# A transformer's opening, regrouped by feature tiles: x first, squares summed on TensorE, six projections fed one tile of x at a time

## The chip, the cores and the metric

One core of a Trainium2 chip runs the whole program. The metric is the device time of one execution in microseconds. TensorE (PE) multiplies, VectorE (DVE) and ScalarE (ACT) do elementwise work, GpSimd (POOL) does a little of it, and SyncE (SP) only issues transfers. "PEld" is the loading of a matmul's stationary operand.

## The reference, cut to what matters

The reference is a chain of transformer layers on 256 rows of 1024 features. Only the first lines of the first layer matter here:

```
cond = silu(c)
mod  = cond @ ada_w[0] + ada_b[0]              # 6 x 1024: shift, scale, gate, ...
shift_m, scale_m, gate_m, ... = split(mod, 6)
h    = rmsnorm(x, g) * (1 + scale_m) + shift_m
proj = h @ attn_w_in[0]                        # qa ka va qb kb vb, 512 wide each
qa, ka = partial_rope(qa, positions), partial_rope(ka, positions)
...                                            # two attentions, output projection, feed-forward, further layers
```

Every weight is used once, so all of them are read from memory in the order of use. `rmsnorm` needs the sum of squares of a row over all 1024 features.

## The kernel before

Activations lie transposed: a tile holds 128 features (partitions) by 256 rows (columns), so x is eight tiles `self.x[k]`, each 128x512, of which the right half is scratch. The list `PLAN` names all weight units in order of use. A unit is up to 128x1024 float32 (512 KB). "mat" units are weights of a projection: ACT writes a rounded copy `h` (L378), DVE the remainder `l` (L379), and `mm3` multiplies with three matmuls per 128x128 block (L405 to L407: weight-high by activation-high, weight-high by activation-low, weight-low by activation-high), each streaming 256 columns. "mod" units are eighths of a modulation vector, stored transposed: one DVE operation (L491) multiplies a 128x1024 unit by the broadcast row `cond` and sums along the row, which gives 128 values as one column.

`pump` issues the loads on SP's queue, up to 12 units ahead, into a ring of nine buffers (`raw`); a buffer is free again when its unit has been used (mod) or split into `h` and `l` (mat). Split units wait in a ring of five. `get` takes the next mat unit, and `flush` works off the mod units that stand ahead of it.

A planner orders the instructions of each engine when the program is built: it issues what its own timing model finds ready, and the program order is only a preference. Semaphores are placed after that, so each engine runs its list strictly in order on the chip.

The opening runs like this. `build` loads the column constants, the broadcast `cond` row (512 KB), the broadcast positions, constants with an all-ones matrix, and x on ACT's queue behind the `cond` activation. `rope_tables` makes sine and cosine on DVE and ACT. `push` squares each x tile on ACT and adds up on POOL and DVE; two matmuls with `ones` finish the sum (L558, L559). `rsq` turns it into 1/rms `r` (two table functions on ACT, three DVE operations). `flush(KT)` works off eight mod units for the scale, `scale` makes x·gain·r (L853), `flush` works off eight more for the shift, `shift` makes the high and low parts of h (L860, L861). Then `moba_proj` makes the projections qa and ka for four head pairs, 24 matmuls each, and rotates each (copy L753, a matmul with `rot1` L755, DVE L756, POOL L757, DVE add, and for q `headsplit`). `vproj` makes va (L413 to L415, 48 matmuls of 512 columns). Attention, the second group and the output projection follow; the feed-forward part begins at about 180 us.

PSUM has eight banks: three tagged "mm", four "ax", one "nm". The tag "u" (four tiles) holds the intermediates of the rope tables and of the rotations.

Of the kernel before, what the change touches and what calls it, by code (L numbers as in the profile page):

```python
# [13 lines left out]
OP = mybir.AluOpType  # L14
# [74 lines left out]
def plan():  # L89
# [81 lines left out]
def _col_plan():  # L171
    o = 0
    for name, n in (("norm_mix_g", 16), ("norm_ffn_g", 16), ("ada_b", 96), ("final_norm_g", 8),
                    ("gdn_conv", 96), ("gdn_norm_g", 1), ("a_log", 1), ("dt", 1),
                    ("b_mod_2", 144), ("ffn1_norm_2", 16), ("mix_norm_2", 16), ("ffn2_norm_2", 16),
                    ("final_norm_2", 8), ("conv_w_2", 12), ("q_norm_2", 6), ("kv_norm_2", 4),
                    ("inv_freq", 1)):
        COLS[name] = (o, n)
        o += n
    return o  # L180
# [5 lines left out]
def pack_cols(i):  # L186
# [5 lines left out]
    def lay(v):  # L192
# [9 lines left out]
        "final_norm_g": _vec(i["final_norm_g"]), "gdn_conv": conv1, "gdn_norm_g": _vec(i["gdn_norm_g"][0]),  # L202
        "a_log": pad(i["gdn_a_log"][0]), "dt": pad(i["gdn_dt_bias"][0]),
        "b_mod_2": lay(i["b_mod_2"]), "ffn1_norm_2": lay(i["ffn1_norm_2"]), "mix_norm_2": lay(i["mix_norm_2"]),
# [6 lines left out]
def constants():  # L211
# [3 lines left out]
    c["ident"] = np.eye(128)  # L215
    c["ones"] = np.ones((128, 128))
    c["triu"] = (p[:, None] <= p[None, :]) * 1.0
# [41 lines left out]
    for g in range(2):  # L259
# [13 lines left out]
CONST = constants()  # L273
CONST_GROUPS = (("ident", "ones", "triu", "half", "rot1"),
                ("tril", "trimid", "upper", "m_causal", "m_sb", "m_lev"),
# [24 lines left out]
class Builder:  # L300
# [59 lines left out]

    def pump(self):
        nc = self.nc
        while self.pd < min(len(PLAN), self.pos + self.LOOK):
# [28 lines left out]
    def flush(self, n=len(PLAN)):  # L392

        end = self.pos + n
        while self.pos < min(end, len(PLAN)) and PLAN[self.pos][0] != "mat":
            self.pump()
            r = self.raw.pop(self.pos)
            self.mod_unit(PLAN[self.pos][1], r)
            self.pos += 1
# [69 lines left out]
    def condition(self, n, t):  # L469
# [4 lines left out]
        return t  # L474

    def conditions(self):

        self.conds[1:] = [self.condition(n, self.t("cnd")) for n in (1, 2)]

    def mod_unit(self, key, r):  # L480
# [12 lines left out]
        if m == KT - 1:  # L493
            o, _ = COLS["ada_b" if ns == 1 else "b_mod_2"]
            nch = 6 if ns == 1 else 9
            b = self.cols[:, o + (l * nch + ch) * 8:o + (l * nch + ch) * 8 + 8]
            for s in range(ns):
                v = t[:, 8 * s:8 * s + 8]
                nc.vector.tensor_tensor(v, v, b, op=OP.add)
                if ns == 2 and ch in (2, 8):  # L500
                    nc.vector.tensor_scalar(v, v, 0.5, None, op0=OP.mult)

    def gain(self, name, l, gname, ch):
# [22 lines left out]

    def stats(self, total=KT, gains=None):


        return {"gains": gains, "acc": None, "first": {}, "n": {}, "total": total, "p": {}}  # L530

    def push(self, st, src, c0, c1):
# [148 lines left out]
    def rope_tables(self):  # L681
        nc = self.nc
        pi = self.t("u", dt=I32)
        nc.scalar.dma_start(pi, bass.AP(tensor=self.a["pos"].tensor, offset=self.a["pos"].offset,
                                        ap=[[0, 128], [1, T]]))
        ang, kk, rr = self.t("u"), self.t("u"), self.t("u")
        nc.vector.tensor_copy(kk, pi)
        o = COLS["inv_freq"][0]
        nc.vector.tensor_scalar(ang, kk, self.cols[:, o:o + 1], None, op0=OP.mult)
        tab = self.t("tab")  # L690
# [52 lines left out]

    def moba_proj(self, h):
        nc = self.nc
        cos, sin = self.rope
        qz, ks = [], []
        for m in range(4):
            pq = self.gemm(self.get(("qa", m)), h, 0, T)
            pk = self.gemm(self.get(("ka", m)), h, 0, T)  # L750
            for p, i in ((pq, 0), (pk, 1)):
                t, u = self.t("u"), self.t("u")
# [12 lines left out]
        self.c = self.load_consts(1, "cst1")  # L765
        return qz, ks, self.vproj("va", h)

# [80 lines left out]

    def scale(self, st, A):

        r = self.rsq(st["p"][0], 1.0 / D)
        for k, x in enumerate(self.x):
            self.nc.vector.scalar_tensor_tensor(x[:, T:], x[:, :T], A[:, k:k + 1], r, op0=OP.mult, op1=OP.mult)  # L853

    def shift(self, B):

        h = [self.pair("h", T) for _ in range(KT)]
        for k, (hi, lo) in enumerate(h):
            t, b = self.x[k][:, T:], B[:, k:k + 1]
            self.nc.scalar.activation(hi, t, AF.Identity, bias=b)  # L860
            self.nc.vector.scalar_tensor_tensor(lo, t, b, hi.bitcast(F32), op0=OP.add, op1=OP.subtract)  # L861
        return h

    def attention(self, B, gate):
        h = self.shift(B)
        qa = self.moba_proj(h)
        P, oa, ob, ze = {}, [], [], {}
# [544 lines left out]
    def build(self):  # L1412
# [4 lines left out]
        right = es1.enter_context(self.tc.tile_pool(name="cond", bufs=1, side="right"))  # L1417
        self.conds = [self.condition(0, right.tile([128, D], F32, name="cond")), None, None]
        self.phase("attn")
        self.rope = self.rope_tables()  # L1420
        g0 = self.load_consts(0, "cst0")
        self.c0 = g0
        self.ident, self.ones, self.triu = g0["ident"], g0["ones"], g0["triu"]
        self.pump()
        self.x = []
        for k in range(KT):
            t = self.xp.tile([128, 512], F32, name=f"x{k}")
            nc.scalar.dma_start(t[:, :T], a["xT"][:, k])
            self.x.append(t)
        self.eps = {}  # L1430
        for e in (EPS, EPS * EPS):
            self.eps[e] = self.keep(1, f"eps{e}")
            nc.vector.memset(self.eps[e], e)
        self.table(LOG_SET)
        st = self.stats()
        for k in range(KT):
# [21 lines left out]
        for l in range(2):  # L1458
# [3 lines left out]
            else:  # L1462
                self.flush(KT)
                self.scale(st, self.gain("ada_w", 0, "norm_mix_g", 1))
                self.flush()
                st = self.attention(self.mod["ada_w", 0, 0], lambda: self.mod["ada_w", 0, 2])
            self.dump(f"x{2 * l}")
# [95 lines left out]
```

## Time and profile before

| | us |
|---|---|
| median of 3 runs | 2498.66 (2496.10 to 2502.42) |
| the profiled execution | 2497.55 |
| its span, first to last instruction | 2495.7 |
| PE busy | 2391.3 (96%) |
| PE weight loads busy | 2130.3 (85%) |
| DVE busy | 1786.3 (72%) |
| ACT busy | 1073.5 (43%) |
| POOL busy | 169.9 (7%) |

The span is split into busy shares by engine, so an average hides stages: here PE is busy nearly all the time except in the first stretch. Matmuls overlap one another in the pipeline, so the distance from start to start, not the duration shown, tells what one costs.

### The profile page before, as it was taken

The numbers are of one execution on the slowest core, as the hardware profiler recorded it, in microseconds if no ns is written. First come the engines' busy times: TensorE is split into PE (matmuls) and PEld (weight loads), VectorE is DVE, ScalarE is ACT, GpSimd is POOL, SyncE is SP. The second block draws the span as 40 slices with busy tenths as digits, with TensorE's granted clock in tenths as the row PEclk, the third lists the DMA queues.
The fourth block names the chain that finished last, engine by engine and source line by source line (L and its number), as shares of the span: only waits on it lengthen the run. The fifth ranks groups of instructions, "written<-read, shape, count | busy, mean of one in ns | idle before, by whom it ended". The sixth has DMA issues, their size and how long they took to land.

```text
span 2495.7 us, 38415 instructions
## 1 busy us (share of the span) xinstructions
PE 2391.3 (96%) x14963; PEld 2130.3 (85%) x14963; DVE 1786.3 (72%) x3087; ACT 1073.5 (43%) x1879; POOL 169.9 (7%) x172
## 2 busy tenths in 40 slices
PE   3999998899999999999999999999999999999998
PEld 2889998898999888888886888888988878988998
DVE  8987779886897997763657597663687663675765
ACT  3554455566644622223537432223432223456444
POOL 1000000414100100000010100000100000111000
PEclk9999999999999999999999999999999999999999
DMA  9766676432786475542220265452365452242652
GB/s 332 271 223 227 225 236 225 153 102 90 263 265 209 161 236 191 173 162 99 79 79 33 85 219 178 153 182 87 109 201 180 160 175 95 83 131 77 205 183 70
DMA packets 118406, 412.21 MB, mean 165 GB/s; under 512 B 13136, under 2 KB 16464, under 8 KB 118224
## 3 DMA queue, kind: packets, MB, share of 16 engines
q1 hardware_dynamic: 113904, 402.28, 47.7%
q10 hardware_dynamic: 4320, 7.47, 0.9%
q8 instruction: 118, 1.93, 0.3%
q14 instruction: 64, 0.52, 0.1%
HBM read 408.66 MB, written 1.05 MB: 164 GB/s over the span
## 4 chain that ended last, share of the span: by engine, by line
PE 76%; DVE 9%; DMA 8%; issue 3%; ACT 2%; POOL 1%; DVEq 0%; ACTq 0%; SPq 0%; POOLq 0%
PE pmm L405 21%; PE pmm L406 21%; PE pmm L407 21%; DMA r<-w 7%; DVE l L379 2%; DVE r L491 2%; DVE junk L491 2%; PE pax L1026 2%; PE pmm L1348 1%; PE pax L407 1%; PE pax L406 1%; PE pax L405 1%; PE pnm L1387 1%; PE pax L1358 1%; ACT h L378 1%
## 5 line engine op out<-in xcount | busy, mean ns | idle before, releaser
L378 ACT CAST h<-r 128x1024 fp32r<-128x1024 f32 (+2 forms) x543 | 549.6, 1017 | 992.4 <-PE pmm L406 907.3
L379 DVE TENSOR_TENSOR l<-r,h 128x1024 fp32r<-128x1024 f32 (+2 forms) x543 | 645.0, 1192 | 195.6 <-ACT h L378 188.2
L405 PE MATMUL pmm<-h,h 128*128 128x512 f32 (+1 forms) x1916 | 668.3, 350 | 31.3 <-ACT h L860 23.1
L406 PE MATMUL pmm<-h,h 128*128 128x512 f32 (+1 forms) x1916 | 664.7, 347 | 1.8 <-DVE h L593 1.6
L407 PE MATMUL pmm<-h,l 128*128 128x512 f32 (+1 forms) x1916 | 662.3, 346 | 0.0
L405 PEld LDWEIGHTS pmm<-h,h 128*128 128x128 f32 x1916 | 364.1, 190 | 78.1 <-ACT h L860 23.8
L406 PEld LDWEIGHTS pmm<-h,h 128*128 128x128 f32 x1916 | 364.2, 190 | 48.5 <-DVE h L593 3.7
L407 PEld LDWEIGHTS pmm<-h,l 128*128 128x128 f32 x1916 | 364.2, 190 | 44.7 <-issue 0.2
L405 PE MATMUL pmm<-hid,h 128*128 128x256 f32 (+1 forms) x1053 | 349.8, 332 | 6.2 <-DVE s L633 2.7
L406 PE MATMUL pmm<-hid,h 128*128 128x256 f32 (+1 forms) x1053 | 348.3, 331 | 1.5 <-DVE hid L444 1.5
L407 PE MATMUL pmm<-hid,l 128*128 128x256 f32 (+1 forms) x1053 | 348.0, 331 | 0.7 <-DVE l L379 0.7
L405 PE MATMUL pmm<-hb,h 128*128 128x258 f32 x1008 | 286.4, 284 | 5.7 <-ACT hb L581 4.2
L407 PE MATMUL pmm<-hb,l 128*128 128x258 f32 x1008 | 284.9, 283 | 0.0
L406 PE MATMUL pmm<-hb,h 128*128 128x258 f32 x1008 | 284.9, 283 | 0.0
L491 DVE SCALAR_TENSOR_TENSOR junk<-r,cnd 128x1024 f32<-128x1024 f32 x144 | 175.9, 1221 | 125.9 <-DMA r<-w 122.6
L405 PEld LDWEIGHTS pmm<-hid,h 128*128 128x128 f32 x1053 | 200.4, 190 | 26.3 <-ACT hid L443 3.9
L406 PEld LDWEIGHTS pmm<-hid,h 128*128 128x128 f32 x1053 | 200.4, 190 | 20.9 <-DVE hid L444 2.4
L407 PEld LDWEIGHTS pmm<-hid,l 128*128 128x128 f32 x1053 | 200.5, 190 | 19.3 <-DVE l L379 1.1
L405 PEld LDWEIGHTS pmm<-hb,h 128*128 128x128 f32 x1008 | 190.8, 189 | 7.3 <-ACT hb L581 5.0
L406 PEld LDWEIGHTS pmm<-hb,h 128*128 128x128 f32 x1008 | 191.7, 190 | 0.4 <-DVE hb L582 0.2
L407 PEld LDWEIGHTS pmm<-hb,l 128*128 128x128 f32 x1008 | 191.7, 190 | 0.1
L491 DVE SCALAR_TENSOR_TENSOR r<-r,cnd 128x1024 f32<-128x1024 f32 x144 | 176.1, 1223 | 5.5 <-ACT cnd L464 2.4
(332 smaller groups left out, 2867.8 us busy)
## 6 DMA issues: line engine op xcount, KB each, us to landing
r<-w SPq DMA_DIRECT2D x665, 512.0 KB, 4.2
r<-w SPq DMA_DIRECT2D x96, 448.0 KB, 3.4
r<-w SPq DMA_DIRECT2D x16, 256.0 KB, 2.5
cnd<-cond ACTq DMA_DIRECT2D x8, 512.0 KB, 4.6
r<-w SPq DMA_DIRECT2D x6, 384.0 KB, 3.2
const<-const SPq DMA_DIRECT2D x2, 960.0 KB, 6.3
x<-xT ACTq DMA_DIRECT2D x8, 128.0 KB, 5.7
x<-ctxT ACTq DMA_DIRECT2D x8, 128.0 KB, 2.6
```

The lines of the kernel that those rows point to most:

```text
L378: nc.scalar.copy(h[:, :n], r[:, :n])
L379: nc.vector.tensor_tensor(lo[:, :n], r[:, :n], h[:, :n].bitcast(F32), op=OP.subtract)
L405: nc.tensor.matmul(out, wh, ah, start=start, stop=False)
L406: nc.tensor.matmul(out, wh, al, start=False, stop=False)
L407: nc.tensor.matmul(out, wl, ah, start=False, stop=stop)
L491: nc.vector.scalar_tensor_tensor(o, r, 1.0, self.conds[ns - 1 + s], op0=OP.mult, op1=OP.mult, accum_out=t[:, 8 * s + m:8 * s + m + 1])
L1026: nc.tensor.matmul(p[:, s], a[:, s], b[:, s], start=True, stop=True)
L1348: self.nc.tensor.matmul(s, q, k, start=True, stop=True)
L1358: self.nc.tensor.transpose(p[:, 128 * b:128 * b + 128], P[:, 128 * b:128 * b + 128], self.ident)
L1387: nc.tensor.matmul(o[64 * a:64 * a + 64, 128 * qt:128 * qt + 128], V[2 * s + b][:, h], pts[a][:, 128 * b:128 * b + 128], start=b == 0, sto ...
```

## The change

The plan's first 24 units become eight groups of three: a mod unit for scale (eighth m), a "modk" unit for shift (all 1024 inputs by 128 outputs, not transposed), and a mat unit "first" m that holds, for feature tile m, the 128x128 blocks of six projections (qa and ka of head pairs 0 to 2). The bytes are the same as before. `first_tiles` walks the eight tiles of x: it works off the two modulation units, makes h for this tile, splits it, and adds the tile's product to all six projections, which stay open in six PSUM banks. `mod_cols` makes the shift column with eight small matmuls (the condition as a 128x32 stationary operand, 128 columns streamed, four column groups of the array), a copy on ACT, a matmul with `ones` and an ACT addition. The squares of x are summed by eight matmuls with `ones`. x·r goes to POOL. The `cond` row and the positions are loaded as single rows and spread over the partitions by matmuls; `ones` is written by a memset; x's loads are issued first, half on each of two queues; the constants of group 0 are loaded at the third tile, and the rope tables come after the six projections. The 24 mod units of the stage that follows are spread over 26 mat units instead of 32.

```diff
 def plan():
-    u = A(0, 1, 0)
     a = "attn_w_in"
-    q = []
+    u, q = [], []
+    for m, scale in enumerate(A(0, 1)):
+        u.append(scale)
+        u.append(("modk", ("ada_w", 0, 0, m), [("ada_w", 0, kt * 128, m * 128, 128) for kt in range(KT)]))
+        u.append(("mat", ("first", m), [(a, 0, m * 128, c + i * 128, 128) for i in range(3) for c in (0, 512)]))
     for s, base in (("a", 0), ("b", 1536)):
-        for m in range(4):
+        for m in range(0 if base else 3, 4):
...
-    u += _evenly(q, A(0, 2, 3, 4), 4, 0)
+    u += _evenly(q, A(0, 2, 3, 4), 2, 0)
...
+    def spread_row(self, p, row):
+        self.nc.tensor.matmul(p, self.ones[0:1, :], row, start=True, stop=True)
...
+    def mod_cols(self, key, r):
...
+        p = self.ax()
+        for kt in range(KT):
+            g = 32 * (kt % 4)
+            nc.tensor.matmul(p[g:g + 32, :128], self.cond0[:, kt, :], r[:, kt * 128:kt * 128 + 128],
+                             start=kt < 4, stop=kt >= 4)
+        e = self.t("u")
+        nc.scalar.copy(e[:, :128], p[:, :128])
+        nc.tensor.matmul(p[:, 256:264], e[:, :128], self.ones[:, :8], start=True, stop=True)
+        o = COLS["ada_b"][0] + m
+        nc.scalar.activation(self.mod[key[:3]][:, m:m + 1], p[:, 256:257], AF.Identity, bias=self.cols[:, o:o + 1])
...
     def push(self, st, src, c0, c1):
+        if st["tensor"]:
+            n = st["n"][0] = st["n"].get(0, 0) + 1
+            if n == 1:
+                st["p"][0] = self.psum("nm", 1)[:, :T]
+            nc.tensor.matmul(st["p"][0], self.ones, s[:, :T], start=n == 1, stop=n == tot)
+            return
...
-    def moba_proj(self, h):
+    def moba_proj(self, st):
+        h, ps = self.first_tiles(st)
+        self.rope = self.rope_tables()
         for m in range(4):
-            pq = self.gemm(self.get(("qa", m)), h, 0, T)
-            pk = self.gemm(self.get(("ka", m)), h, 0, T)
-            for p, i in ((pq, 0), (pk, 1)):
+            if m == 3:
+                ps += [self.gemm(self.get((n, m)), h, 0, T) for n in ("qa", "ka")]
+            for p, i in ((ps[2 * m], 0), (ps[2 * m + 1], 1)):
...
+    def first_tiles(self, st):
         r = self.rsq(st["p"][0], 1.0 / D)
+        for x in self.x:
+            nc.gpsimd.tensor_tensor(x[:, T:], x[:, :T], r, op=OP.mult)
+        ps = [(self.ax if i % 2 else self.mm)()[:, :T] for i in range(6)]
+        h = []
         for k, x in enumerate(self.x):
+            self.flush()
+            t, (hi, lo) = self.t("t"), self.pair("h", T)
+            nc.scalar.activation(t, x[:, T:], AF.Identity, scale=self.scale0[:, k:k + 1],
+                                 bias=self.mod["ada_w", 0, 0][:, k:k + 1])
+            h.append(self.split(t, hi, lo))
+            u = self.get(("first", k))
+            if k == 2:
+                self.c0.update(self.load_consts(0, "cst0"))
+                self.ident, self.triu = self.c0["ident"], self.c0["triu"]
+            for i, p in enumerate(ps):
+                self.mm3(p, u, i, hi, lo, k == 0, k == KT - 1)
+        return h, ps
...
 def build(self):
+        rows = [self.t("og")[0:1, :] for _ in range(2)]
+        for i in range(2):
+            nc.scalar.dma_start(rows[i], a["cond"][0:1, 512 * i:512 * i + 512])
+        self.x = []
+        for k in range(KT):
+            t = self.xp.tile([128, 512], F32, name=f"x{k}")
+            (nc.sync if k % 2 else nc.scalar).dma_start(t[:, :T], a["xT"][:, k])
+            self.x.append(t)
+        self.pump()
+        for i in range(2):
+            p = self.mm()
+            self.spread_row(p, rows[i])
+            self.act(self.conds[0][:, 512 * i:512 * i + 512], p, AF.Silu)
...
         self.table(LOG_SET)
-        st = self.stats()
+        st = self.stats(tensor=True)
```

## Rows read from the trace of the kernel before

**Rows 1.** The page: busy tenths of PE, DVE and DMA in 40 equal slices.
```profile
PE   3999998899999999999999999999999999999998
DVE  8987779886897997763657597663687663675765
DMA  9766676432786475542220265452365452242652
```

**Rows 2.** The chain that ended last, opening: start, duration, what.
```profile
7.48 5.15 DMA x<-xT
...
32.15 1.14 DVE r L491 x2
...
43.97 0.09 DVE mod_ada_w L499
44.08 0.52 ACT h L860
44.64 1.01 PE pmm L405 x3
```

**Rows 3.** Busy time by stretch: PE, PEld, DVE, ACT, POOL, PEclk, DMA share, GB/s.
```profile
0.00:44.64 44.64, 2.07 (x4) 1.17 (x4) 33.05 (x70) 13.61 (x22) 4.97 (x9) 1.00 0.95 351
20.00:35.00 15.00, 1.55 (x4) 0.67 (x2) 14.57 (x34) 5.07 (x8) 0.00 (x0) 1.00 1.03 411
44.64:49.30 4.66, 4.66 (x20) 4.38 (x21) 4.66 (x10) 3.68 (x8) 0.00 (x0) 1.00 0.91 323
49.30:73.17 23.87, 23.87 (x189) 23.25 (x188) 23.23 (x37) 10.70 (x18) 6.05 (x6) 1.00 0.89 324
73.17:84.90 11.73, 11.73 (x52) 9.47 (x51) 11.03 (x18) 5.19 (x7) 2.20 (x2) 1.00 0.91 302
84.90:180.00 95.10, 89.58 (x681) 82.28 (x679) 83.64 (x161) 51.93 (x99) 4.38 (x5) 1.00 0.63 227
```

**Rows 4.** DVE by line, 8.9 to 44.64 us: busy, mean ns, idle before.
```profile
L491 DVE SCALAR_TENSOR_TENSOR r<-r,cond 128x1024 f32<-128x1024 f32 x16 | 19.4, 1216 | 8.0 <-DMA r<-w 8.0
L379 DVE TENSOR_TENSOR l<-r,h 128x1024 fp32r<-128x1024 f32 x4 | 4.8, 1216 | 0.0
L853 DVE SCALAR_TENSOR_TENSOR x<-x,gain_ada_w,r 128x256 f32<-128x256 f32 x8 | 3.2, 474 | 0.0
L491 DVE DVE_READ_ACCUMULATOR r<-r,cond 128x1 f32 x16 | 1.3, 80 | 0.0
```

**Rows 5.** By stretch, instructions on tile u alone (rope tables).
```profile
0.00:44.64 44.64, 0.00 (x0) 0.00 (x0) 6.54 (x17) 0.83 (x2) 0.00 (x0) 1.00 0.95 351
```

**Rows 6.** ACT and POOL by shape, 0 to 200 us.
```profile
L860 ACT ACTIVATE h<-x,mod_ada_w 128x256 fp32r<-128x256 f32 x8 | 3.3, 494 | 6.1 <-DVE mod_ada_w L499 6.1
L464 ACT ACTIVATE y<-pnm,eps1e-06_155 128x256 f32<-128x256 f32 x2 | 1.0, 476 | 0.0
L757 POOL TENSOR_TENSOR u<-u,tab 128x256 f32<-128x256 f32 x8 | 8.3, 1031 | 48.7 <-PE pax L755 48.6
```

**Rows 7.** The chain, 66 to 185 us: full float32 matmuls of 256 columns.
```profile
66.31 0.43 PE pax L755 x2
...
183.39 0.85 PE pnm L558 x2
```

**Rows 8.** Busy time by stretch around the end of attention.
```profile
180.00:182.40 2.40, 0.09 (x2) 0.01 (x1) 2.40 (x5) 2.40 (x7) 1.03 (x1) 1.00 0.91 314
182.40:186.00 3.60, 3.60 (x13) 3.24 (x14) 3.60 (x12) 3.57 (x9) 0.00 (x0) 0.53 0.64 228
```

**Rows 9.** PE in order of time: six float32 matmuls, two column groups.
```profile
99.91 0.43 PE L739 MATMUL pax<-pt,v 128*64 128x128 f32 x2
...
100.67 0.38 PE L741 MATMUL pax<-pt,v 128*64 128x128 f32 x2
100.98 0.33 PE L803 MATMUL pax<-const,pz 128*128 128x128 f32 x1
```

**Rows 10.** Opening in order of time: the first weight unit's use.
```profile
8.93 1.23 DVE L491 SCALAR_TENSOR_TENSOR r<-r,cond 128x1024 f32<-128x1024 f32 x1 [8.03 <-DMA r<-w]
```

More of the change, by code (lines that the diff above doesn't have):

```diff
@@ L273 @@
 CONST = constants()
-CONST_GROUPS = (("ident", "ones", "triu", "half", "rot1"),
+CONST_GROUPS = (("ident", "triu", "half", "rot1"),
                 ("tril", "trimid", "upper", "m_causal", "m_sb", "m_lev"),
@@ L358, in ax, with pump @@
         return self.psum("ax", 4)
-    def pump(self):
+    def pump(self, look=LOOK):
         nc = self.nc
-        while self.pd < min(len(PLAN), self.pos + self.LOOK):
+        while self.pd < min(len(PLAN), self.pos + look):
             n, i = WIDTH[self.pd], self.pd
@@ L492, in mod_unit @@
                                            accum_out=t[:, 8 * s + m:8 * s + m + 1])
-        if m == KT - 1:
+        if key[:3] == ("ada_w", 0, 1):
+            o, g = COLS["ada_b"][0] + KT + m, COLS["norm_mix_g"][0] + m
+            nc.vector.scalar_tensor_tensor(self.scale0[:, m:m + 1], t[:, m:m + 1], self.bias1[:, m:m + 1],
+                                           self.cols[:, g:g + 1], op0=OP.add, op1=OP.mult)
+        elif m == KT - 1:
             o, _ = COLS["ada_b" if ns == 1 else "b_mod_2"]
@@ L501, in mod_unit @@
                     nc.vector.tensor_scalar(v, v, 0.5, None, op0=OP.mult)
+    def mod_cols(self, key, r):
+        nc = self.nc
+        m = key[3]
+        if m == 0:
+            self.mod[key[:3]] = self.keep(KT, "mod_first")
+        p = self.ax()
[8 more added lines that the diff above has]
+        nc.scalar.activation(self.mod[key[:3]][:, m:m + 1], p[:, 256:257], AF.Identity, bias=self.cols[:, o:o + 1])
     def gain(self, name, l, gname, ch):
@@ L525, in rsq, with stats @@
         return r
-    def stats(self, total=KT, gains=None):
-        return {"gains": gains, "acc": None, "first": {}, "n": {}, "total": total, "p": {}}
+    def stats(self, total=KT, gains=None, tensor=False):
+        return {"tensor": tensor, "gains": gains, "acc": None, "first": {}, "n": {}, "total": total, "p": {}}
     def push(self, st, src, c0, c1):
@@ L683, in rope_tables @@
         pi = self.t("u", dt=I32)
[L684 to L685 removed]
+        nc.scalar.dma_start(pi[0:1, :], self.a["pos"])
         ang, kk, rr = self.t("u"), self.t("u"), self.t("u")
[L687 removed]
+        nc.vector.tensor_copy(kk[0:1, :], pi[0:1, :])
+        p = self.ax()[:, :T]
+        self.spread_row(p, kk[0:1, :])
         o = COLS["inv_freq"][0]
[L689 removed]
+        nc.vector.tensor_scalar(ang, p, self.cols[:, o:o + 1], None, op0=OP.mult)
         tab = self.t("tab")
@@ L847, in sb_weights, with attention @@
         self.act(z, z, AF.Exp)
-    def scale(self, st, A):
+    def first_tiles(self, st):
+        nc = self.nc
         r = self.rsq(st["p"][0], 1.0 / D)
+        for x in self.x:
+            nc.gpsimd.tensor_tensor(x[:, T:], x[:, :T], r, op=OP.mult)
+        ps = [(self.ax if i % 2 else self.mm)()[:, :T] for i in range(6)]
+        h = []
         for k, x in enumerate(self.x):
[L853 to L866, printed above, removed]
+            self.flush()
[10 more added lines that the diff above has]
+        return h, ps
+    def attention(self, st, gate):
+        qa, h = self.moba_proj(st)
         P, oa, ob, ze = {}, [], [], {}
@@ L1417, in build @@
         right = es1.enter_context(self.tc.tile_pool(name="cond", bufs=1, side="right"))
-        self.conds = [self.condition(0, right.tile([128, D], F32, name="cond")), None, None]
         self.phase("attn")
[L1420 to L1429, printed above, removed]
+        self.ones = self.keep(128, "ones")
+        nc.gpsimd.memset(self.ones, 1.0)
+        self.cond0 = self.t("og")[:, :32 * KT].rearrange("p (k c) -> p k c", k=KT)
+        nc.gpsimd.memset(self.cond0, 0.0)
         self.eps = {}
@@ L1433, in build @@
             nc.vector.memset(self.eps[e], e)
+        rows = [self.t("og")[0:1, :] for _ in range(2)]
[7 more added lines that the diff above has]
+        self.pump()
+        self.conds = [right.tile([128, D], F32, name="cond"), None, None]
+        for i in range(2):
+            p = self.mm()
+            self.spread_row(p, rows[i])
+            self.act(self.conds[0][:, 512 * i:512 * i + 512], p, AF.Silu)
+        o = COLS["c"][0]
+        self.act(self.cond0[:, :, 0], self.cols[:, o:o + KT], AF.Silu)
+        self.scale0, self.bias1 = self.keep(KT, "scale0"), self.keep(KT, "bias1")
+        o = COLS["ada_b"][0] + KT
+        nc.vector.tensor_scalar(self.bias1, self.cols[:, o:o + KT], 1.0, None, op0=OP.add)
+        self.c0 = {}
         self.table(LOG_SET)
-        st = self.stats()
+        st = self.stats(tensor=True)
         for k in range(KT):
@@ L1462, in build @@
             else:
[L1463 to L1466, printed above, removed]
+                st = self.attention(st, lambda: self.mod["ada_w", 0, 2])
             self.dump(f"x{2 * l}")
```

9 lines of the change are left out of this document (4 added, 5 removed).

## The prediction, made before the change was run

> **What bounds the kernel now.** I read the page's busy tenths first: PE is at 8 or 9 in every slice but the first, where it is at 3 while DVE and DMA are at 8 and 9 [rows 1]. So the program is PE's, apart from one hole at its start. The chain of waits shows what the hole consists of: x lands at 12.6, then squares, DVE's modulation products, and the last of them (L499) frees ACT's first h at 44.08 and PE's first projection at 44.64 [rows 2]. The stretches say who works meanwhile: up to 44.64 PE is busy 2.07 us, DVE 33.05 [rows 3]; DVE's idle time is nearly all before its first product at 8.93, the landing of the first weight unit [rows 4, 10]. From there DVE is the limit, with 16 products (19.4 us) and the rope tables (6.54) [rows 4, 5]. Transfers run at 411 GB/s at most, 351 in the mean [rows 3]. From 44.64 on PE has no gap until 84.90, and up to 180 only 5.5 us; DVE is almost as full there, 23.23 of 23.87, then 11.03 of 11.73, then 83.64 of 95.10 [rows 3]. That second fact decides how much of an earlier start survives.
>
> **The change part by part: what must land.** The bytes of the first 24 units are 2816 columns per group, 1.44 MB, eight groups 11.5 MB. Ahead of them stand the column constants (0.23 MB) and x (1.05 MB); the 512 KB `cond` row, the 128 KB positions and 257 KB of constants ahead of the units are gone or moved. Before, 0.23 + 0.26 + 0.51 + 0.13 MB and the first unit, 1.64 MB, were in at 8.93 [rows 10]. Now 1.80 MB precede the same moment, 0.16 MB more, 0.4 us at 411 GB/s: first unit at 9.3, x complete at about 8. SP's queue issues four x loads ahead of its first unit; that is in this shift. One group takes 3.52 us at 411 GB/s; the third unit of group 0 lands at 11.5, of group 7 at 36.6 with the 0.2 MB of constants moved behind group 2. By before's mean of 351 GB/s the 12.9 MB take 36.7, the same. The ring of nine holds three groups, and its oldest unit must be used before the tenth load goes; DVE, which frees it, needs per group one product (1.22 + 0.08), a remainder of 768 columns (0.9, from the 1.22 of 1024), the low part of h (about 0.4, as L853's) and a gain column, together 2.7 us against 3.52 [rows 4]. So transfers are not held back.
>
> **The sum of squares.** Before, POOL and DVE added. Now PE does, eight float32 matmuls of 256 columns: 0.43 each at the upper level of the clock, 0.85 at the lower [rows 7]. From the landing of the first x (about 5.5) they end at 9 to 13; I take the lower level, 13. The two spreads of the `cond` row, 512 columns, cost by the same rows 0.85 to 1.7 each and lie before, while x is on its way; without that cover they would add 3.4. Then `rsq`: five dependent operations at most 0.48 each [rows 6], 2.5 with hand-overs: r at 15.5. POOL's first x·r takes 0.8 to 1.03 [rows 6], ACT's two operations 0.49 each [rows 6]: first projection matmul at 17.3, against 44.64. POOL's other seven at 1.03 stay ahead of PE. The extra table loads of ACT lie in its idle time (13.61 busy of 44.64 [rows 3]).
>
> **The eight groups on PE.** 18 matmuls per group; 189 records take 23.87 [rows 3]; seven rotations among them (14 records) are 3.0 by [rows 7], so the others are 0.12 each: 2.16 per group, 17.3 in all. Before, the first 20 took 4.66 instead of 2.4 [rows 3]; PE has now worked before, so I add 1. The shift columns are new on PE and the trace has no such matmul. The nearest: six float32 matmuls of 128 columns in two column groups take 1.07 us from 99.91 to 100.98, 0.18 each [rows 9]. Eight are 1.4 if four groups help no more than two, 0.7 if twice as much, and 1.7 if they help nothing (half of 0.43 each [rows 7]). I take 0.9, plus 0.2 for the matmul with `ones`; groups 0 and 1 are done while PE waits for r, six remain: 6.6. That gives 17.3 + 17.3 + 1 + 6.6 = 42.2. The transfers allow it: modk of group 7 lands at 35.7, then matmuls 0.9, ACT copy 0.3, matmul 0.3, column 0.2, three operations for h 1.3, hand-overs 0.4, together 3.4, then 2.16: 41.3. **Six projections end at 42** (bounds 41 and 47).
>
> **What that is worth.** Left on PE after them: two projections 5.8, eight rotations at 0.43, va 11 (its 48 matmuls in the stretch of 11.73): 20.1. Before, va ended at 84.90, so the six projections stood, in equal terms, at 64.8. PE alone would gain 22.8 us.
>
> DVE does not allow all of it. To 180 us it was busy 33.05 + 4.66 + 23.23 + 11.03 + 83.64 = 155.6 [rows 3]. Eight products leave it (half of 19.4 + 1.3, 10.35), L853 (3.2) goes to POOL, an addition of 0.4 to PE; eight small columns come (1.3): 142.9. By 42 us it can have done 8 products 10.4, 8 remainders 7.2, the low parts 3.2, small ones 2.5, three remainders ahead 3.6 and the rope tables 6.5 [rows 4, 5]: 33.4 in the 32.7 us since 9.3. So it is full too, and 109 remain. At the shares of the later stretches, 0.88 to 0.97 [rows 3], these take 112 to 124 us: end of attention at 154 to 166 instead of 180. I take a share of 0.9, since the 24 products now sit on 26 units: 42 + 121 = 163. **17 us gained.** From 180 on the units and their order are unchanged and PE sets the time, so the shift stays. 2497.55 - 17 = 2480.5; the median of the runs shown stands 1.1 above the profiled time. What a measurement tells from no change is about 0.3%, 7.5 us.
>
> **The clock.** After 2.3 us without matmuls at 180, the granted clock is 0.53, the 1.2 GHz level, for 3.6 us, where before and after it is 1.00, the 2.4 GHz level [rows 8]. A gap of that length in each group would double PE's price. The Trainium skill ("TensorE: Matmul & The Clock Gate", section "HAM oscillation — how this bites in real kernels") says that a loop over K-tiles that waits for a transfer in each falls to the lower level in every one; [rows 8] agree in kind, and by that rule this opening would be the third rival below. With 3.1 us of PE work per 3.52 us and three groups waiting when r arrives, I expect no such gaps.
>
> **The rivals.** *DVE takes more of it.* The rope tables share the four "u" tiles with the shift columns and stand behind them in program order; if they run only after group 7, 6.5 us of DVE and ACT's sines hold the first rotation, and through it the PSUM banks that the next projections need. At a share of 0.88 attention ends at 166, with up to half of the tables uncovered at 166 to 170: 10 to 14 gained, 2484 to 2488. For it: DVE has no slack in either stretch. Against: it interleaved tables and products before [rows 4, 5].
>
> *No gaps, but group by group.* If the planner leaves each shift column behind the projections of the previous group, a group takes 2.16 + 3.4 = 5.6 and the six end at 17.3 + 8 x 2.16 + 7 x 3.4 = 58: 6.5 gained on PE, 2491.
>
> *The same at the lower clock, the other sign.* Then PE is idle some 2.5 us in each group, as long as the gap in [rows 8]. Its work doubles: 4.2 for the projections (18 at 0.23, the first 20 of before in 4.66 [rows 3]), about 4.3 for the column's way (0.9 more): the six end at 17.3 + 8 x 4.2 + 7 x 4.3 = 81, 16 us late: 2514. It is slower than before from 5.95 us per group on, measurably from 6.9. Against it: one "ax" bank, the matmuls' order and the loads leave room for the next column under the projections, and PE's list in attention is strongly interleaved.
>
> *More than forecast.* DVE at 0.97, with PE's 22.8: 2473 to 2475.
>
> **How the numbers follow.** Forecast 0.60, with its own range 2475 to 2485; DVE takes more 0.22; group by group 0.05; at the lower clock 0.08; more than forecast, or an end below 2473, 0.05. The range 2472 to 2492 leaves out the lower clock, half of group by group and a little below: 0.13 or so. Faster by over 0.3% (under 2491): the forecast 0.60, 0.19 of the second, half of the group-by-group 0.02, and the last 0.05, together 0.86; within 0.3% the rest of those, 0.06; slower 0.08.
>
> **What would show each step.** First projection matmul at 16 to 19; six projections' last matmul at 41 to 47; va's end at 62 to 68; first feed-forward matmul at about 165 instead of 182.4 [rows 8]; DVE busy over 90% from 9 to 160; granted clock 1.00 from 17 on. Eight shift matmuls at 0.7 to 1.4 together. The prediction is wrong if the clock is near 0.5 between 17 and 45, if rope tables begin after 38, if r comes after 20, or if the spacing of matmuls behind 165 differs from before's.

## The result, and the profile after

The changed kernel takes 2518.22 us (median of 4 runs, 2515.58 to 2520.69), beside it the kernel before 2497.72 (4 runs): a ratio of 1.0068, interval 1.0053 to 1.0082. By that ratio it is slower by 17 us (20.5 by the medians, 18.1 by the profiled spans), where 17 us less were forecast. The spans are 2513.8 and 2495.7.

The page's busy tenths, and the granted clock:

```profile
PE   6799998899999999999999999999999999999998
DVE  4988779976898898673557497673677673585765
PEclk8899999999999999999999999999999999999999
```

Against [rows 1] the hole in PE's first slice is half filled, 6 for 3, but the second slice has a new one, 7 for 9. DVE's first slice fell from 8 to 4: the engine that was the limit now waits.

Busy time by stretch, after: up to the first projection matmul (28.34), to the end of the second group (42.15), to the six projections' end (65.5), to va's end (100.2), to the first feed-forward matmul (200.1). The columns are those of [rows 3].

```profile
0.00:28.34 28.34, 12.15 (x38) 5.76 (x39) 7.78 (x18) 13.12 (x25) 3.10 (x10) 0.95 0.84 297
28.34:42.15 13.81, 11.37 (x88) 9.42 (x88) 9.56 (x14) 4.52 (x11) 5.74 (x5) 0.60 0.71 233
42.15:65.50 23.35, 19.55 (x183) 17.53 (x183) 13.76 (x23) 13.16 (x28) 0.00 (x0) 0.93 0.90 318
65.50:100.20 34.70, 23.39 (x114) 19.29 (x114) 31.66 (x62) 12.75 (x22) 8.39 (x8) 0.85 0.69 246
100.20:200.10 99.90, 92.85 (x683) 84.46 (x681) 86.48 (x166) 54.63 (x105) 5.42 (x5) 0.96 0.64 225
```

The same stages before (to the point that equals the six projections' end, to va's end, to the first feed-forward matmul):

```profile
0.00:64.80 64.80, 22.23 (x145) 20.68 (x146) 52.57 (x102) 23.48 (x39) 8.23 (x13) 1.00 0.92 332
64.80:84.90 20.10, 20.10 (x117) 17.60 (x116) 19.39 (x31) 9.70 (x15) 4.99 (x4) 1.00 0.95 346
84.90:182.40 97.50, 89.67 (x682) 82.30 (x680) 86.04 (x165) 54.33 (x105) 5.41 (x5) 1.00 0.64 229
```

So the opening gains nothing (65.5 against 64.8), the stage behind it takes 14.6 more (34.7 against 20.1), the next 2.4 more, and 17.7 us stay to the end: from the first feed-forward matmul to the end of the span it is 2313.3 before and 2313.7 after. DVE did 31.1 us by 65.5 after, 52.6 by 64.8 before.

What PE does up to the first feed-forward matmul, before and after; and, summed, the stretches of the kernel after in which the granted clock is 0.50, the 1.2 GHz level (25.7 to 39.3, 59.8 to 63.2, 73.5 to 83.7 and 107.6 to 114.4):

```profile
0.00:182.40 182.40, 132.00 (x941) 120.57 (x941) 158.00 (x296) 87.51 (x157) 18.64 (x22) 1.00 0.77 278
0.00:200.10 200.10, 159.30 (x1103) 136.46 (x1103) 149.24 (x279) 98.19 (x187) 22.65 (x27) 0.91 0.71 250
sum 34.00, PE 22.76 PEld 18.76 DVE 24.99 ACT 14.61 POOL 10.54; mean PE 5.69 PEld 4.69 DVE 6.25 ACT 3.65 POOL 2.63
```

PE's idle time fell by 9.6 us (50.4 to 40.8), but its busy time grew by 27.3, and that makes the 17.7. The growth is 162 more records, the new small matmuls, and 22.8 us of work at the lower level; at half the clock that costs up to 11.4, an estimate (half of 22.76). The kernel before shows 1.00 in every stage up to 182.4. For its first 20 projection matmuls that does not fit: they took 0.23 each [rows 3], as the first ones after do at 0.50 (0.21).

**The late start.** After, in order of time: SP's and ACT's first instructions, the first square, the first product; PE's list up to r; what makes r.

```profile
1.18 3.05 SPq L1477 DMA_DIRECT2D x<-xT  x4
4.28 7.75 SPq L368 DMA_DIRECT2D r<-w  x9
8.35 1.28 ACT L453 ACT_TABLE_LOAD   x1
9.65 0.72 ACT L564 ACTIVATE sq<-x 128x256 f32<-128x256 f32 x2
11.32 1.23 DVE L497 SCALAR_TENSOR_TENSOR r<-r,cond 128x1024 f32<-128x1024 f32 x1 [7.40 <-DMA r<-w]
...
12.92 0.60 PE L523 MATMUL pax<-r,og 128*32 128x128 f32 x2 [5.32 <-DMA r<-w]
13.45 2.08 PE L573 MATMUL pnm<-sq,ones 128*128 128x256 f32 x4
...
21.43 0.47 ACT L466 ACTIVATE y<-pnm,eps1e-06_88 128x256 f32<-128x256 f32 x1 [0.79 <-PE pnm L573]
21.94 0.42 ACT L466 ACTIVATE y<-y 128x256 f32<-128x256 f32 x1
22.37 1.28 ACT L453 ACT_TABLE_LOAD   x1
23.67 0.83 ACT L380 CAST h<-r 128x768 fp32r<-128x768 f32 x1
24.41 0.41 ACT L549 ACTIVATE r<-y 128x256 f32<-128x256 f32 x1
25.41 0.42 DVE L552 SCALAR_TENSOR_TENSOR r<-a,r 128x256 f32<-128x256 f32 x1
25.90 4.17 POOL L892 TENSOR_TENSOR x<-x,r 128x256 f32<-128x256 f32 x5 [24.71 <-DVE r L552]
...
28.34 0.58 PE L407 MATMUL pmm<-h,h 128*128 128x256 f32 x1 [6.94 <-ACT h L445]
```

Four x loads stand on SP's queue for 3.05 us, of which the last one waits 1.3 for an x load to land, so the first weight unit is issued at 4.28 instead of 1.66 and its product starts at 11.32 instead of 8.93. ACT squares only from 9.65 on, behind table loads and the `cond` activations. PE's list puts a shift matmul (L523), which waits for a weight unit, ahead of the first sum (L573): PE starts at 12.92, though two squares were done by 10.4. Then ACT's table load and a weight cast stand between the exponential and the next step of r, and on DVE a product and a remainder stand ahead of r's last operation (25.41). PE waits from 21.39 to 28.34.

**The groups.** One group in the steady part, from the shift column of the next tile to its first projection matmul:

```profile
52.32 0.29 PE L527 MATMUL pax<-ones,u 128*128 128x8 f32 x2
52.64 0.26 ACT L529 ACTIVATE mod_first<-pax,cols 128x1 f32<-128x1 f32 x1 [1.73 <-PE pax L527]
52.95 0.65 PE L523 MATMUL pax<-r,og 128*32 128x128 f32 x16 [0.35 <-ACT mod_first L529]
52.98 0.60 ACT L898 ACTIVATE t<-x,mod_first,scale 128x256 f32<-128x256 f32 x1
53.62 0.40 ACT L445 CAST h<-t 128x256 fp32r<-128x256 f32 x1
54.07 0.39 PE L407 MATMUL pmm<-h,h 128*128 128x256 f32 x1 [0.47 <-ACT h L445]
```

L527 stands behind the projections of the tile before, so column, t and h (1.75 us) follow one another with PE idle 0.35 and 0.47. What is in this way is what the second rival described, at a lower price.

**The rope tables.** Their first and last steps, and PE's next rotation (L792):

```profile
63.33 0.27 DVE L720 CAST u<-u 1x256 f32<-1x256 int32 x1
...
77.65 0.42 ACT L466 ACTIVATE tab<-u 128x256 f32<-128x256 f32 x1 [2.45 <-DVE u L738]
...
79.81 1.65 PE L792 MATMUL pax<-u,const 128*128 128x256 f32 x3 [9.45 <-ACT u L790]
```

The load of the positions needs a "u" tile and those go round with the shift columns: it is issued at 57.68. The tables' short operations then share DVE with products of 1.2 us, and PE stands still for 9.45 us.

### The profile page after: what moved, and what is told of

It reads as the page before. It is cut to its first block, busy times and chain, and to the rows that moved or that the text cites. A ratio compares the mean times of both kernels' runs of the same rounds, so it can differ in the third digit from the quotient of the medians.

```text
span 2513.8 us, 38772 instructions
## 1 busy us (share of the span) xinstructions
PE 2419.4 (96%) x15125; PEld 2148.7 (85%) x15125; DVE 1777.6 (71%) x3070; ACT 1083.6 (43%) x1909; POOL 173.1 (7%) x177
## 4 chain that ended last, share of the span: by engine, by line
PE 79%; DVE 8%; DMA 7%; issue 3%; ACT 2%; POOL 1%; DVEq 0%; SPq 0%; ACTq 0%; POOLq 0%
PE pmm L408 22%; PE pmm L407 22%; PE pmm L409 21%; DMA r<-w 7%; DVE l L381 2%; DVE r L497 2%; PE pax L1070 1%; PE pax L409 1%; PE pax L408 1%; PE pax L407 1%; PE pmm L1392 1%; DVE junk L497 1%; PE pnm L1431 1%; PE pax L1402 1%; ACT h L380 1%
## 5 line engine op out<-in xcount | busy, mean ns | idle before, releaser
L380 ACT CAST h<-r 128x1024 fp32r<-128x1024 f32 (+3 forms) x545 | 549.8, 1014 | 984.2 <-PE pmm L408 904.6
L381 DVE TENSOR_TENSOR l<-r,h 128x1024 fp32r<-128x1024 f32 (+3 forms) x545 | 645.5, 1189 | 202.7 <-ACT h L380 193.3
L407 PE MATMUL pmm<-h,h 128*128 128x512 f32 (+1 forms) x1892 | 661.0, 350 | 16.8 <-ACT h L445 9.6
L408 PE MATMUL pmm<-h,h 128*128 128x512 f32 (+1 forms) x1892 | 658.7, 348 | 2.7 <-DVE h L627 1.6
L409 PE MATMUL pmm<-h,l 128*128 128x512 f32 (+1 forms) x1892 | 655.5, 347 | 0.0
L407 PEld LDWEIGHTS pmm<-h,h 128*128 128x128 f32 x1892 | 359.9, 191 | 65.5 <-ACT h L445 11.8
L408 PEld LDWEIGHTS pmm<-h,h 128*128 128x128 f32 x1892 | 360.2, 190 | 48.9 <-DVE h L627 3.7
L407 PEld LDWEIGHTS pmm<-hid,h 128*128 128x128 f32 x1053 | 200.4, 190 | 25.8 <-ACT hid L445 3.2
```

Of the source, the lines that this page charges most:

```text
L380: nc.scalar.copy(h[:, :n], r[:, :n])
L381: nc.vector.tensor_tensor(lo[:, :n], r[:, :n], h[:, :n].bitcast(F32), op=OP.subtract)
L407: nc.tensor.matmul(out, wh, ah, start=start, stop=False)
L408: nc.tensor.matmul(out, wh, al, start=False, stop=False)
L409: nc.tensor.matmul(out, wl, ah, start=False, stop=stop)
```

## The experiments

Milestones from each trace (us): first projection matmul, end of the six projections, first feed-forward matmul; and the ratio to the kernel before, with its interval, from runs side by side on one chip. 0.001 is 2.5 us.

```
run                           first  six end    ffn   ratio (95%)
before                        44.64   (64.8)  182.4
after                         28.34    65.5   200.1   1.0068 (1.0053-1.0082)
rope_early                    28.55    67.4   187.3   1.0032 (1.0017-1.0048)
stats_first                   22.51    67.5   198.4   1.0056 (1.0039-1.0072)
shift_ahead                   26.45    60.2   193.2   1.0072 (1.0055-1.0088)
three_edits                   28.82    61.1   182.4   1.0011 (0.9998-1.0025)
squares_early                 27.34    58.5   180.7   0.9983 (0.9974-0.9992)
scale_on_pe                   26.28    67.4   185.5   1.0027 (1.0014-1.0039)
no_rope_work                  22.07    55.4   176.8   0.9984 (0.9972-0.9995)
no_shift_matmuls              23.68    51.3   174.4   0.9994 (0.9977-1.0011)
half_shift_bytes              24.05    51.6   174.9   0.9983 (0.9967-0.9999)
no_scale_products             25.24    58.5   181.4   1.0008 (0.9995-1.0022)
rope_after_first              21.46    57.4   179.7   1.0004 (0.9992-1.0017)
..._cols_behind               21.37    61.3   184.7   1.0029 (1.0016-1.0041)
```

**rope_early.** The tables' DVE work ahead of the norm's table load, with tiles of its own; the sines stay.

```diff
-        pi = self.t("u", dt=I32)
+        pi = self.t("rt", dt=I32)          # ang, kk, rr too; "rt": (256, 5)
...
+        self.rope_args()                   # ahead of the opening's first table load
```

> The changed kernel with one edit: the rope tables' DVE work is written ahead of the table load for the norm and has tiles of its own; the two sines stay where they were. Theory (three waits in the opening add up: a late 1/rms, groups that stand in a row, rope tables that come last): the 9.5 us in which PE waits for the first rotated copy vanish, with the lower clock behind them, so 10 to 14 us less than the changed kernel's 2518: 2504 to 2508, and the first rotation follows the six projections within 2 us. Rival (DVE is full from 9 us on, so its 6.5 us only move and hold the groups instead): at most 3 us less, 2515 or more.

Measured 2505.63 us. The stall is gone, DVE is full where PE had stood still; the stretch from 70 to 80 us:

```profile
70.00:80.00 10.00, 8.26 (x52) 7.26 (x52) 10.00 (x18) 4.08 (x8) 4.55 (x5) 1.00 0.91 346
```

Against 0.55 us of PE work there after. The feed-forward part starts 12.8 earlier and the end comes 9 (by the ratios) to 12.6 us (by the medians) earlier: more than half of the loss.

**stats_first.** The shift matmuls ordered behind the last sum.

```diff
+            self.after(i, self.last_stat)      # i: each L523 matmul
```

> The changed kernel with one edit: PE's list has all eight matmuls that sum the squares ahead of the first shift matmul. Theory: PE no longer waits for the shift weights (5.3 us before 12.92) with squares ready from 10.4 on; the sum ends 3 to 4 us earlier, near 17.5 instead of 21.4, the first projection matmul comes at 23 to 25 instead of 28.3, and the end moves by as much, 3 to 5 us: 2513 to 2515. Rival (the weights that land set the pace of the groups, not the start of the first): first matmul earlier, end within 1.5 us of the changed kernel's.

Measured 2513.81, in the expected range; but by the ratios that is 3 us less than the changed kernel, which the intervals do not tell from nothing, and it did not come the expected way. The first projection came 5.8 earlier and the six projections ended 2 later. In its trace the rope row's spread (L480) stands in PE's list ahead of the last group:

```profile
62.23 1.19 PE L480 MATMUL pax<-u,ones 1*128 1x256 f32 x2 [4.45 <-DVE u L721]
```

**shift_ahead.** The next tile's columns ahead of this tile's projections, so that PE covers their way.

```diff
+            if k < KT - 1:
+                self.flush()
             for i, p in enumerate(ps):
                 self.mm3(p, u, i, hi, lo, k == 0, k == KT - 1)
```

> The changed kernel with one edit: the modulation units of group k+1 are worked off in the program ahead of the projection matmuls of group k. Theory (groups stand in a row because the matmul that finishes a shift column stands behind the previous group's 18 matmuls in PE's list): the steady group of 4.0 us falls to about 3.0 to 3.5, the six projections end 4 to 7 us earlier, the end by the same: 2511 to 2514. Rival (DVE or the landing of the weights sets the 4.0 us): group stays at 4.0, no difference beyond 1.5 us.

Measured 2517.89, no gain. The six projections ended 5.3 earlier (1.9 of it by an earlier first projection) and the feed-forward part began 6.9 earlier, so the mechanism held; the gain is lost further on (the distance from the first feed-forward matmul to the end of the span is 2323.0 against 2313.7). Behind that matmul both traces hold the same instructions in the same order on every engine that computes. PE is busy 6.6 us longer here and idle 2.7 longer, and the granted clock falls to 0.50 in four more stretches. About the same place of the list, in the changed kernel and here:

```profile
1074.30:1077.70 3.40, 3.40 (x17) 2.82 (x16) 2.00 (x6) 0.95 (x1) 0.00 (x0) 1.00 0.56 189
1067.40:1070.80 3.40, 3.40 (x9) 2.65 (x8) 3.37 (x7) 0.45 (x1) 0.00 (x0) 0.50 0.29 106
```

In the same time PE gets through 9 matmul records at 0.50 and 17 at 1.00.

**three_edits.** All three.

> The three edits together (early rope tables, sum of squares ahead of the shift matmuls on PE, shift of the next group ahead of this group's projections). Theory: the gains add up, 17 to 25 us less than the changed kernel: 2493 to 2501, level with or a little under the kernel before. Rival (DVE is the limit once PE's waits are gone): the sum falls short, 2503 or more, with DVE over 95% busy from 10 to 100 us.

Measured 2502.94, between the two expectations. The feed-forward part starts exactly where it did before. r was still at 24.5. DVE is full from 60 on (29.59 of the 30 us to 90):

```profile
60.00:75.00 15.00, 13.45 (x82) 11.90 (x81) 14.63 (x23) 6.41 (x13) 6.33 (x6) 0.97 0.86 285
```

**squares_early.** A fourth edit: squares and sums written ahead of the loop that starts the weights.

```diff
+        st = self.stats(tensor=True)
+        for k in range(KT):
+            self.push(st, self.x[k], 0, T)
         self.pump()
```

> The three edits and a fourth: the squares and their sums are written ahead of the loop that starts the weight units, so that on ACT and PE they stand ahead of the first cast and of the shift matmuls. Theory (the late r still costs PE, one for one up to the landing of the last groups): r at 17 to 19 instead of 24.5, first projection matmul at 20 to 22 instead of 28.82, the six projections' end at 52 to 54 instead of 59, va's end at 77 to 80 instead of 83.7, and 2502.9 falls by 4 to 7, to 2496 to 2499. Rival (DVE is full from 58 on and sets va's end whatever PE does before): va's end at 82 to 84 and 2501 to 2503.

Measured 2498.26 beside 2502.8 for the kernel before; by the ratios 7 us less than with three edits, the upper end of what was expected. It is the only complete version with an interval below 1, by less than the 0.3% that the prediction takes for no change. The way there is not the one expected: the sums end at 14, but r's last operation stands on DVE behind operations on the angles, a product and a remainder, and ends at 24.5; the first projection is at 27.34, and va ends at 81.9, where the rival had 82 to 84. Its stages:

```profile
0.00:27.34 27.34, 13.44 (x58) 7.37 (x58) 11.13 (x26) 15.49 (x29) 3.42 (x10) 0.82 0.89 310
27.34:58.46 31.12, 27.12 (x253) 24.24 (x254) 21.14 (x40) 17.19 (x37) 4.21 (x5) 0.83 0.82 288
58.46:81.90 23.44, 20.64 (x113) 17.50 (x112) 23.44 (x38) 9.80 (x18) 8.74 (x8) 1.00 0.85 296
81.90:180.70 98.80, 92.22 (x683) 84.48 (x681) 91.87 (x177) 54.95 (x105) 6.74 (x5) 0.97 0.71 252
```

DVE is busy 32.3 of the first 58.46 us and then 115.3 of 122.2. In the eight groups PE is busy 27.1 of 31.1 us, at a mean granted clock of 0.83. Of the 4.0 idle, 3.3 are one wait for the low part of h (L446), which stands behind operations on the angles on DVE:

```profile
PE pmm L408 <- DVE h L446: 3.3, 1, 3.3
```

**scale_on_pe** moves DVE's eight scale products to PE, made as the shift columns are.

```diff
-    for m, scale in enumerate(A(0, 1)):
-        u.append(scale)
+    for m in range(KT):
+        u.append(("modk", ("ada_w", 0, 1, m), ...))
```

> The four edits, and the scale columns too are computed as the shift columns are, by eight small matmuls, so that DVE loses eight 1024-column products (8 x 1.3 = 10.4 us) and PE gets 8 x 0.65 to 1.1 = 5 to 9 us. If DVE sets the time between the six projections and va's end, va ends 5 to 8 earlier than with four edits, and the end is 3 to 7 earlier, 2490 to 2496. If PE or the landings set it, the six projections end 3 to 6 later and the end is the same or up to 5 later, 2497 to 2503.

Measured 2509.33: 11 more than with four edits in runs side by side, more than either theory allowed. DVE is free (18.94 of 41.12) and the eight groups take 41.1 us instead of 31.1. So DVE's scale products are not the limit of the opening.

**no_rope_work.** The angles' work left out, nothing in its place.

> The four edits, with DVE's work on the rope angles left out (and the positions' load and spread); the two sines are taken of ones, so the rotation angles are not the reference's. It takes some 6.5 us from DVE and nothing else. If DVE is the limit from 58 on, va's end and the end are 4 to 6 earlier than with four edits, 2491 to 2494. If DVE has room by then, 0 to 1.

Measured 2498.49, as with four edits. The first projection is at 22.07, the eight groups take 33.3 us instead of 31.1, the feed-forward part begins 3.9 earlier, and the end does not come earlier.

**no_shift_matmuls, half_shift_bytes, no_scale_products** ask what sets the groups' pace.

```diff
-            i = nc.tensor.matmul(p[g:g + 32, :128], self.cond0[:, kt, :], ...)   # first: all of the column's work
-            nc.sync.dma_start(t[:, :n], ...)                                     # second: half of a modk unit
+            nc.sync.dma_start(t[:, :512], ...)
-            nc.vector.scalar_tensor_tensor(o, r, 1.0, self.conds[ns - 1 + s], ...)  # third: the scale products
+            nc.vector.tensor_copy(t[:, m:m + 1], r[:, :1])
```

> The four edits, with the shift columns' work left out (eight small matmuls, ACT's copy and the matmul with ones of each group; the column is taken from the first column of the weight unit, so it is not the reference's); every unit is still loaded. With four edits the eight groups take 31 us, from 27.3 to 58.5, where the forecast had 24.9. If the column's way on PE and ACT sets their pace, that becomes 22 to 25 and the six end at 49 to 53. If the landings set it, or the ring that lets the next load go, 29 to 31 and 56 to 58.

> The four edits, with only the first half of each of the eight shift units loaded (the eight matmuls read that half twice, so the columns are not the reference's): 0.26 of 1.44 MB less in each group, 2.1 MB or some 6 us at 330 GB/s in all, and no work less on any engine. If the landings set the groups' pace, the eight groups take 25 to 28 us instead of 31. If the column's way on PE sets it, 30 to 31.

> The four edits, with the eight scale products on DVE left out (8 x 1.3 us; a copy of one column stands in for each, so the scale is not the reference's); every unit is still loaded. If DVE, which lets go of a third of the ring's slots, sets when the next load can go, the eight groups take 25 to 28 us instead of 31, and va ends 5 to 8 earlier than 81.9. If not, 30 to 31 and va ends within 2 of it.

Measured 2498.53, 2498.16 and 2502.70 (before 2500.42). The eight groups, in this order:

```profile
23.68:51.26 27.58, 21.69 (x145) 19.81 (x146) 21.83 (x41) 15.32 (x30) 4.71 (x5) 0.92 0.92 335
```
```profile
24.05:51.57 27.52, 25.57 (x253) 22.92 (x254) 23.99 (x45) 18.30 (x38) 4.77 (x6) 0.94 0.84 302
```
```profile
25.24:58.48 33.24, 28.02 (x253) 24.24 (x254) 16.04 (x34) 17.55 (x38) 4.29 (x5) 0.87 0.80 279
```

Either the columns' work or their bytes taken away ends the six projections 7 earlier, half of it by an earlier first projection; the groups take 27.5 instead of 31.1, where 22 to 25 and 25 to 28 were expected. 5.1 us of DVE's work taken from the same groups (16.04 for 21.14) ends the six at the same 58.5, so the scale products do not set the pace. That the landings do is not shown: in the groups of these four traces no engine waits for a landing. Of the 3.6 us that half_shift_bytes gains in the groups, 1.6 is PE's busy time for the same 253 records (25.57 for 27.12) at a granted clock of 0.94 for 0.83, and the rest is idle time: the wait of 3.3 for the low part of h is not there. Behind the groups DVE is busy all the time, 23.44 of 23.44 with four edits.

**rope_after_first** writes the angles' work behind the first group, so that r is early; **rope_after_first_cols_behind** leaves out shift_ahead as well.

```diff
+            if k == 1:
+                self.rope_args()
```

> The four edits, with the rope tables' DVE work (own tiles, own load and spread) written behind the first group of projections instead of ahead of r. With four edits three operations on the angles and their spread stand ahead of r's last operation on DVE and PE: r at about 25, first projection matmul at 27.34, and at 22.07 where the angles were left out. Expected: first projection matmul at 21.5 to 23, six projections' end at 54 to 57 instead of 58.5, first feed-forward matmul at 177 to 179 instead of 180.7. At the end, by a shift that is passed on whole, 2 to 4 less than with four edits; by the runs in which 6 us at the feed-forward start left nothing, the same within 2.

> As the run before, without the shift columns' move ahead of the projections (so the planner's own order of the columns). If the move is worth its 0.5 to 0.9 us in each group, the six projections end 3 to 6 later than in that run and the end is 0 to 5 later; if the landings set the pace, both are the same within 1.

Measured 2503.61 and 2511.43 (before 2503.0). A first projection earlier by 5.9 us brought the six projections' end forward by 1.1 only, with the angles' work now among the groups; without that work, in no_rope_work, 5.3 earlier brought 3.1. What PE waited for from 20 to 58 us (total, times, longest):

```profile
PE pmm L407 <- ACT h L445: 8.6, 7, 3.3
```

h is late in seven groups. In the first it waits for r, the longest wait (3.3); in the others, 5.3 together, it stands in ACT's list behind its shift column and what is mixed in there, casts of weights and a table load. At the end this version is 5 us later than with four edits (by the ratios), though its feed-forward part begins 1.0 earlier. The move of the columns is worth 3.9 at the six projections' end, as expected, and 6 to 8 at the end, a little more.

## Why the prediction was wrong

Three terms of the sum failed: r at 15.5, the eight groups' 24.9, and the rope tables' 6.5 us counted as done by 42. With them came the gaps at the lower clock that were not expected. The signs of being wrong that the prediction names came too: r after 20, tables after 38, a clock near 0.5 between 17 and 45.

**r, and with it the first projection.** Forecast 15.5 and 17.3, measured 25.8 and 28.34: 11.0 late. The first sum of squares was costed from x's landing, as if PE and ACT were free then; in their lists stood shift matmuls, table loads and activations (the sum ended at 21.4 instead of 13). `rsq` took 4.4 instead of 2.5: the table loads were said to lie in idle time, and one lies between its operations, with a cast on ACT and a product and a remainder on DVE. The first unit was shifted by bytes alone, 0.4 us; four x loads ahead of it on SP's queue cost 2.6. stats_first, squares_early and rope_after_first each brought the first projection forward; in rope_after_first, at 21.46, it ended the six projections only 1.1 earlier, so r is not the whole of it.

**The shift column's price was right:** 0.65 at the upper level of the clock, 1.08 at the lower, for 0.9.

**The groups.** Forecast 24.9, measured 37.2. The sum has 5.3 for the first two, twice 2.16 and 1 for the clock; they take 13.8 (28.34 to 42.15). The clock is 0.60 there, after PE's wait of 6.95, PE is idle 2.4, and three sets of shift matmuls stand in the stretch (from 33.69, 36.11 and 41.03). Two columns were counted as done while PE waits for r, and one was. For the other six the sum has 3.3 each (2.16 and 1.1), and they take 3.9; PE is idle 3.8 of their 23.35, in gaps such as the 0.35 and 0.47 shown above. The third rival's mechanism is there, for two groups. The Trainium skill ("TensorE: Matmul & The Clock Gate", section "HAM oscillation — how this bites in real kernels") describes a loop that waits for a transfer in each tile and falls to the lower level in every one. The first wait, of 6.95 us, agrees; from 42.15 to 65.50, with gaps of 0.3 to 1.3 us, the mean granted clock is 0.93 and falls to 0.50 once (59.8 to 63.2), so this loop did not fall in every group.

**"So transfers are not held back" failed as well**, but it is not what the engines waited for. Transfers ran at 233 GB/s from 28 to 42 us, where 411 was assumed, and SP waited for the ring's users (from 0 to 62: total, times, longest):

```profile
SPq L368 <- DVE l L381: 13.8, 6, 3.8
SPq L368 <- PE pax L523: 11.8, 7, 4.1
```

A ring of nine is three groups; while r is missing, these stand in it. I had counted DVE's work per group against the landing, not that its users are queued behind r and behind the shift columns on PE. But in the same time the kernel before waits for its ring too (12.8 for L379, 7.5 for L491). And from 9 to 65.5 us a landing ends only PE's first wait (5.3) and DVE's first (7.4). After these, DVE waits for ACT and ACT for PE's columns:

```profile
DVE l L381 <- ACT h L380: 10.3, 8, 3.1
ACT mod_first L529 <- PE pax L527: 8.8, 7, 2.5
```

That is also why **"so it is full too"** failed: DVE did 31.1 us by the end of the six projections, near the 33.4 forecast, but by 65.5 and not by 42.

**"I expect no such gaps"** failed twice: PE waits 6.95 us for the first h and 9.45 for the tables, and the granted clock is 0.50 behind each. The up to 11.4 us that the lower level costs before the feed-forward part lie inside the terms above, in the groups and behind the tables. The third rival's 2514 is near the measured time, but by luck: it had this in every group and no stall of the tables.

**The rope tables** were the first rival, with its mechanism and place; its price was 3 to 7 us above the forecast, measured 9 to 13 (rope_early). It assumed up to half of the tables' 6.5 us uncovered; spread between products of 1.2 us they took from 63.3 to 78.1, and PE stood still for 9.45, until 79.81. The lower clock behind the stall was not in its price.

**What an earlier end of the six is worth.** Behind them 109 us of DVE work at a share of 0.9 were forecast; squares_early shows 115.3 at 0.94, 122.2 us for 121. The total was right by luck, since the two misses cancel; that DVE is nearly full there held. So the opening decides. With four edits the six still end at 58.5 instead of 42, 10.0 of it by the late first projection and 6.2 in the groups, and the feed-forward part starts at 180.7, 1.7 us earlier than before.

**"The shift stays"** holds for the change itself (17.7 at 182.4, 18.1 at the end). Among the experiments up to 7 us of an earlier start are lost behind it: no_shift_matmuls starts the feed-forward part 8.0 before the kernel before and ends within 0.3% of it; rope_after_first starts it 2.7 earlier and ends level. The rows under shift_ahead show most of where: the same instructions in the same order as in the changed kernel, and a granted clock that falls more often. The records of all runs agree. The mean granted clock of a whole run is 0.991 to 0.993 in the median for the kernel before and 0.984 to 0.988 for every changed version, and 0.001 of the clock is about 2.5 us: two runs of the kernel before on one chip, at 0.994 and 0.989, take 2495.73 and 2507.83. So part of what each version won went to the clock, in the opening and in stages that no edit touched. Why it falls more often there is not shown.

## What to carry to other kernels

An early landing is worth what stands first in each engine's list: follow the path instruction by instruction through the lists of ACT, DVE and PE, and count table loads and other units' work among its steps. When work is regrouped so that every group needs a small chain (column, activation, cast), price the chain and the ring slots that wait for it, not the engines' sums. And short work that a later stage needs (here 6.5 us of tables) must not be written last with tiles that the regrouped loop uses: that alone was more than half of the loss. Where PE is the limit, read the granted clock of every stage beside its busy time: 9.6 us less of idle time won nothing here, because PE had more work and part of it ran at the lower level.

## What the runs showed of the hardware

Eight float32 matmuls with a 128x32 stationary operand and 128 columns in four column groups (16 records) take 0.65 us at a granted clock of 1.00 and 1.06 to 1.08 at 0.50.

On SP's queue each load of 128 KB of x is issued in 0.33 to 0.43 us and the first weight unit, 512 KB, in 0.43, so a load is not cheaper to issue for being small. The rest of the four x loads' 3.05 us is the last one's wait for an x load to land:

```profile
SPq L1477 <- DMA x<-xT: 1.3, 1, 1.3
4.28 0.43 SPq L368 DMA_DIRECT2D r<-w  x1
```

While POOL multiplies x by r (until 31.55 in squares_early), DVE's four operations with a scalar on the angles, from 27.96 to 30.97, take 0.81 us each; the next one takes 0.28:

```profile
28.70 0.81 DVE L732 TENSOR_SCALAR rt<-rt 128x256 f32<-128x256 f32 x1
31.76 0.28 DVE L734 TENSOR_SCALAR rt<-rt 128x256 f32<-128x256 f32 x1
```

The prediction moved x·r to POOL at no cost to DVE.
